# A mixture-of-experts kernel: moving one more store behind the last load, cutting the last weight load into whole rows, and storing the last result in one piece

## The chip, the cores and the metric

The kernel runs on one core of a Trainium2 chip. The time is the device time of one execution in microseconds (us); the figure before the change is the median of four runs. One further execution was profiled, and all durations below are from that one.

## The reference

Eight experts, each with its own tokens, weights and biases. Everything is float32.

```python
# x (8, 256, 512)  w1 (8, 512, 2048)  w2 (8, 2048, 512)  b1 (8, 2048)  b2 (8, 512)
def reference(x, w1, w2, b1, b2):
    h = np.matmul(x, w1) + b1[:, np.newaxis, :]
    h = np.maximum(h, 0)
    return (np.matmul(h, w2) + b2[:, np.newaxis, :]).astype(np.float32)
```

## The kernel before

For each expert e the kernel forms a hidden layer and then an output. `first_product(e)` (L108) multiplies `w1` with the transposed tokens in 16 blocks of 128 hidden rows, four matmuls each, and ScalarE applies bias and ReLU into `hT[e]` in fp16. `second_product(e)` (L151) starts two accumulators of 128 tokens x 512 columns with the bias `b2` and adds 16 hidden blocks (j = 0 to 15) to each. `store` (L134) copies the first accumulator to SBUF on VectorE and the second on ScalarE.

The main loop (L243) runs stages s = 0 to 10: stage s computes the first product of expert s and the second product of expert s - 3 (`LAG`). So stage 8 has the second product of expert 5, stage 9 that of expert 6 and stage 10 that of expert 7; these three stages have no first product.

**The ring.** All weight loads, the later token loads and seven of the eight stores are issued by GpSimd (POOL) into one DMA queue, q0, in the order of the list `ring` (L221 to L241). The loads change float32 into fp16 on the way. `flush(e)` (L130) issues the store of a finished expert, 512 KB, from that same list. The issue instruction of a flush waits on POOL until both copies of that expert are done, and everything later in the list waits behind it. There are eight semaphores for these transfers in turn, so each issue also waits until the eighth transfer before it has landed.

The end of the list before the change is: the load of w2 of expert 6 in two halves of 1 MB, flush 3, then the w2 of expert 7 in eight pieces (L232 to L236), then flush 5 and flush 6. Flush 4 stands behind the first piece (L237, L238), because expert 4 is not in `LATE = (5, 6)`. The eight pieces cover these rows j and columns: 0-4, 4-7, 7-10 and 10-12 over all 512 columns, then 12-14 and 14-16 over columns 0 to 320, then 12-14 and 14-16 over columns 320 to 512. A row is 512 float32 numbers in memory and 512 fp16 numbers (1 KB) in SBUF per partition, so a whole-row piece has one contiguous stretch per partition, and a column piece has one stretch per row and partition.

Expert 7 has four accumulators instead of two: columns 0 to 320 in two of them, columns 320 to 512 in two others. When rows 14-16 of the first 320 columns have been added, `store` copies these and SyncE (SP) issues a store of 320 KB (L149). The other 192 columns follow as two stores of 96 KB, one on SyncE (L142) and one on ScalarE's queue (L143). These three go through other DMA queues, q1 (SyncE) and q10 (ScalarE).

Output tiles of 512 columns rotate over three buffers (L48); those of the last expert have buffers of their own.

Of the kernel before, what the change touches and what calls it, by code (L numbers as in the profile page):

```python
# [11 lines left out]
def kernel(  # L12
# [9 lines left out]
    nc = tc.nc  # L22
    fp32 = mybir.dt.float32
    fp16 = mybir.dt.float16
    E, T, H = x.shape
    M = w1.shape[2]
    P = 128
    nTB = T // P
    nKC = H // P
    nJ = M // P  # L30
    HL = 320
    LAG = 3
    LATE = (5, 6)
    RING = (0, 1, 2, 3, 4) + LATE
    PARTS = {}
    nXF32 = 2

    def ordered(ins):
        return tc.keep_in_program_order(ins)

    singles = ctx.enter_context(tc.tile_pool(name="singles", bufs=1))
    w1_pool = ctx.enter_context(tc.tile_pool(name="w1", bufs=3))
    w2_pool = ctx.enter_context(tc.tile_pool(name="w2", bufs=3))
    w2t_pool = ctx.enter_context(tc.tile_pool(name="w2t", bufs=1))
    x_pool = ctx.enter_context(tc.tile_pool(name="xp", bufs=4))
    xT_pool = ctx.enter_context(tc.tile_pool(name="xTp", bufs=2))
    hT_pool = ctx.enter_context(tc.tile_pool(name="hT", bufs=LAG + 2))
    out_pool = ctx.enter_context(tc.tile_pool(name="outp", bufs=3))  # L48
    psum_x = ctx.enter_context(tc.tile_pool(name="psum_x", bufs=1, space=bass.MemoryType.PSUM))
    psum_h = ctx.enter_context(tc.tile_pool(name="psum_h", bufs=3, space=bass.MemoryType.PSUM))  # L50
    psum_o = ctx.enter_context(tc.tile_pool(name="psum_o", bufs=2, space=bass.MemoryType.PSUM))
# [3 lines left out]
    ones1 = singles.tile([1, P], fp16)  # L55
    b2_sb = singles.tile([1, E * H], fp16)
# [6 lines left out]
    w2_sb = [None] * E  # L63
    hT = [None] * E
# [14 lines left out]
    def load_w2(e):  # L79
        src = w2[e].rearrange("(p j) h -> p j h", j=nJ)  # L80
        w2_sb[e] = []
        t = w2_pool.tile([P, nJ, H], fp16, tag="w2", name="w2sb")
        step = nJ if e < E - 2 else nJ // 2
        for lo in range(0, nJ, step):
            ordered(nc.gpsimd.dma_start(out=t[:, lo : lo + step, :], in_=src[:, lo : lo + step, :]))  # L85
            w2_sb[e].append((lo, lo + step, 0, H, t[:, lo : lo + step, :]))

    def load_w2_piece(e, lo, hi, c0, c1):
        t = w2t_pool.tile([P, hi - lo, c1 - c0], fp16, tag=f"w2_{lo}_{c0}", name=f"w2_{lo}_{c0}")
        src = w2[e].rearrange("(p j) h -> p j h", j=nJ)  # L90
        ordered(nc.gpsimd.dma_start(out=t, in_=src[:, lo:hi, c0:c1]))  # L91
        if w2_sb[e] is None:
            w2_sb[e] = []
        w2_sb[e].append((lo, hi, c0, c1, t))

    def transposes(e):
        pt = psum_x.tile([P, nKC, T], fp16, tag="psx", name="psx")
# [33 lines left out]
        dst, src = pending.pop(e)  # L131
        ordered(nc.gpsimd.dma_start(out=dst, in_=src))  # L132

    def store(e, po, c0, c1, split):  # L134
        w = c1 - c0
        pool = out_pool if w == H else singles
        out_sb = pool.tile([P, nTB, w], fp32, tag=f"out{c0}_{w}", name=f"out{w}")
        nc.vector.tensor_copy(out=out_sb[:, 0, :], in_=po[0])  # L138
        nc.scalar.copy(out=out_sb[:, 1, :], in_=po[1])  # L139
        dst = out[e].rearrange("(p tb) h -> p tb h", tb=nTB)[:, :, c0:c1]  # L140
        if split and c1 == H:
            nc.sync.dma_start(out=dst[:, 0, :], in_=out_sb[:, 0, :])  # L142
            nc.scalar.dma_start(out=dst[:, 1, :], in_=out_sb[:, 1, :])  # L143
        elif e in RING:
            pending[e] = (dst, out_sb)
        else:
            step = P // PARTS.get(e, 1)
            for lo in range(0, P, step):
                nc.sync.dma_start(out=dst[lo : lo + step], in_=out_sb[lo : lo + step])  # L149

    def second_product(e):  # L151
        if e < E - 1:
            blocks = [(0, H, psum_o, "po")]
        else:
            blocks = [(0, HL, psum_o, "po"), (HL, H, psum_h, "ph")]
        acc = {}
        for c0, c1, pool, tag in blocks:
            for tb in range(nTB):
                t = pool.tile(
                    [P, c1 - c0], fp32, tag=tag if tag == "ph" else f"{tag}{tb}", name=f"acc{tb}"  # L160
                )
                acc[c0, tb] = t
                ordered(nc.tensor.matmul(  # L163
                    out=t,
                    lhsT=ones1,
                    rhs=b2_sb[0:1, e * H + c0 : e * H + c1],
                    start=True,
                    stop=False,
                ))
        for lo, hi, p0, p1, t in w2_sb[e]:  # L170
            mine = [b for b in blocks if p0 <= b[0] and b[1] <= p1]
            for tb in range(nTB):
                for j in range(lo, hi):
                    for c0, c1, _, _ in mine:
                        ordered(nc.tensor.matmul(  # L175
                            out=acc[c0, tb],
                            lhsT=hT[e][:, j, tb * P : (tb + 1) * P],
                            rhs=t[:, j - lo, c0 - p0 : c1 - p0],
                            start=False,
                            stop=(j == nJ - 1),  # L180
                        ))
            if hi == nJ:
                for c0, c1, _, _ in mine:
                    store(e, [acc[c0, tb] for tb in range(nTB)], c0, c1, e == E - 1)

    x32 = singles.tile([P, nXF32, nTB, H], fp32)
    for e in range(nXF32):
# [4 lines left out]
        out=b2_sb,  # L192
        in_=b2.rearrange("e h -> (e h)").rearrange("(o f) -> o f", o=1),
# [10 lines left out]
    for j in range(nJ):  # L204
        for s in range(2):
            ordered(nc.tensor.matmul(  # L206
                out=pb[s * 64 : (s + 1) * 64, j, :, :],
                lhsT=b1_rows.rearrange("r (q j) -> r q j", j=nJ)[:, :, j],
                rhs=ident[0 : 2 * E, 0 : 2 * E],
                start=True,  # L210
                stop=True,
            ))
    for s in range(2):
        nc.vector.tensor_copy(  # L214
            out=b1T[s * 64 : (s + 1) * 64, :, :], in_=pb[s * 64 : (s + 1) * 64, :, :, s]
# [5 lines left out]
    ring = []  # L221
    for s in range(1, E + LAG - 1):
        if s < E:
            if s >= nXF32:
                ring.append((s - 2, load_x, (s,)))
            ring.append((s - 2, load_w1, (s,)))
        if s >= LAG:
            ring.append((s - 2, load_w2, (s - LAG,)))
        if s >= 2 * LAG:
            ring.append((s - 2, flush, (s - 2 * LAG,)))  # L230
    e = E - LAG - 1
    for piece in (  # L232
        (0, 4, 0, H), (4, 7, 0, H), (7, 10, 0, H), (10, 12, 0, H),
        (12, 14, 0, HL), (14, 16, 0, HL), (12, 14, HL, H), (14, 16, HL, H),
    ):
        ring.append((0, load_w2_piece, (E - 1,) + piece))  # L236
        if e in RING and e not in LATE:  # L237
            ring.append((e + LAG + 1, flush, (e,)))  # L238
            e += 1
    for e in LATE:  # L240
        ring.append((e + LAG + 1, flush, (e,)))  # L241

    for s in range(E + LAG):  # L243
        while ring and ring[0][0] <= s:
            _, put, args = ring.pop(0)
            put(*args)
        if s < E:
            first_product(s)
        if s >= LAG:
            second_product(s - LAG)  # L250
# [31 lines left out]
```

## Time and profile before

| what | value |
|---|---|
| median of 4 runs | 183.58 us (183.32 to 183.65) |
| the profiled execution, its own time | 183.52 us |
| its span, first to last instruction | 181.7 us |
| TensorE matmul busy | 137.5 us (76% of the span) |
| ScalarE busy | 62.8 us (35%) |
| VectorE busy | 13.3 us (7%) |
| packets of DMA queue q0 | 97.8% of 16 engines' span |
| mean TensorE clock granted | 0.927 |

The span is the time from the first to the last instruction on the core; the execution's own time is 1.8 us longer. A core has 16 DMA engines that work for all queues; the share of a queue says how much of their time its packets took. The rate in GB/s counts the bytes of a transfer at its SBUF (or output) side, so a load that halves float32 into fp16 reads twice that from memory. "us to landing" of a DMA is the time from the start of its issue instruction to its last completion count.

### The profile page before, as it was taken

Reading aid. Unit: us, or ns where it says so; the run is one execution under the profiler, and the core shown is the slowest. Engines: PE = TensorE matmul, PEld = TensorE weight load, DVE = VectorE, ACT = ScalarE, POOL = GpSimd, SP = SyncE. Lnnn points to the kernel's source line nnn. Section 1 sums busy time; section 2 is a strip of 40 time slices with the busy share of each in tenths; the row PEclk is TensorE's granted clock in tenths of the full one; section 3 lists DMA queues with packets and bytes.
Section 4 is the critical chain, followed back from the end, with each engine's and each line's share of the span. In section 5 each row is a group of like instructions: output and inputs, shape, how many; then the busy total and the mean of one; then the engine's idle time right before and its main releaser. Section 6 shows DMA issues by size and latency. Waiting matters only on the chain.

```text
span 181.7 us, 2204 instructions
## 1 busy us (share of the span) xinstructions
PE 137.5 (76%) x946; PEld 98.2 (54%) x946; DVE 13.3 (7%) x22; ACT 62.8 (35%) x138; POOL 22.1 (12%) x46
## 2 busy tenths in 40 slices
PE   0545969488380999749992999709999996999790
PEld 0534959488360855737482755708549642434570
DVE  0320101001000101010100101001010010101010
ACT  0022869568270330806063330903309601010000
POOL 7100030300200010111010000200004003113300
PEclk9999999999966599988999699985999999999997
DMA  5989998999899999999999999999899989999995
GB/s 178 294 177 233 231 224 180 209 252 215 191 231 227 213 195 231 197 225 213 231 227 184 224 231 227 177 285 216 191 231 218 283 191 278 211 243 284 216 281 188
DMA packets 7017, 40.58 MB, mean 223 GB/s; under 512 B 1216, under 2 KB 2256, under 8 KB 4960
## 3 DMA queue, kind: packets, MB, share of 16 engines
q0 software_dynamic: 5872, 38.81, 97.8%
q1 hardware_dynamic: 688, 0.95, 1.6%
q10 hardware_dynamic: 448, 0.69, 1.0%
q8 instruction: 7, 0.11, 0.2%
q14 instruction: 2, 0.02, 0.0%
HBM read 71.39 MB, written 4.19 MB: 416 GB/s over the span
## 4 chain that ended last, share of the span: by engine, by line
DMA 82%; PE 13%; POOL 2%; issue 1%; ACT 0%; POOLq 0%
DMA w2sb<-in_w_dram 39%; DMA x<-in_x_dram 24%; DMA w1sb<-in_w_dram 13%; PE ph L113 7%; DMA w<-in_w_dram 6%; PE acc L175 5%; PE psx L100 1%; POOL w1sb L75 1%; PE acc L163 0%; POOL b_sb L191 0%; POOL ident masks.py:199 0%; POOL w2sb L85 0%; POOL ident masks.py:197 0%; ACT out L139 0%; POOLq L266 0%
## 5 line engine op out<-in xcount | busy, mean ns | idle before, releaser
L113 PE MATMUL ph<-xT,w1sb 128*128 128x256 f16 x512 | 68.5, 300 | 11.8 <-DMA w1sb<-in_w_dram 11.8
L120 ACT ACTIVATE hT<-ph,b1T 128x256 f16<-128x256 f32 x128 | 57.0, 474 | 44.4 <-PE ph L113 44.1
L113 PEld LDWEIGHTS <-w1sb 128*128 128x128 f16 x512 | 61.7, 149 | 17.9 <-DMA w1sb<-in_w_dram 12.8
L175 PE MATMUL acc<-w2sb,hT 128*128 128x512 f16 x224 | 49.6, 379 | 1.6 <-DMA w2sb<-in_w_dram 1.6
L175 PEld LDWEIGHTS <-hT 128*128 128x128 f16 x288 | 27.1, 98 | 32.7 <-issue 6.6
L139 ACT COPY out<-acc 128x512 f32<-128x512 f32 (+2 forms) x9 | 4.9, 542 | 59.6 <-PE acc L175 59.6
L100 PE MATMUL psx<-ident,x 128*128 128x128 f16 x64 | 6.6, 264 | 18.6 <-DMA x<-in_x_dram 17.9
L100 PEld LDWEIGHTS <-x 128*128 128x128 f16 x64 | 5.1, 127 | 19.6 <-DMA x<-in_x_dram 18.8
L75 POOL DMA_DIRECT2D w1sb<-in_w_dram x8 | 4.4, 553 | 59.5 <-PE ph L113 58.7
L106 DVE COPY xT<-psx 128x1024 f16<-128x1024 f16 x8 | 5.5, 691 | 82.2 <-PE psx L100 82.2
L138 DVE COPY out<-acc 128x512 f32<-128x512 f32 (+2 forms) x9 | 5.7, 632 | 73.3 <-PE acc L175 73.3
L85 POOL DMA_DIRECT2D w2sb<-in_w_dram x8 | 4.3, 536 | 49.4 <-PE acc L175 49.4
L175 PE MATMUL acc<-w,hT 128*128 128x320 f16 (+1 forms) x64 | 7.8, 272 | 1.4 <-DMA w<-in_w_dram 1.3
L206 PE MATMUL pb<-ident,b_rows 16*64 16x16 f32 x64 | 3.7, 265 | 6.5 <-DMA b_rows<-in_b_dram 6.5
L206 PEld LDWEIGHTS pb<-ident,b_rows 16*64 16x64 f32 x64 | 3.6, 198 | 6.4 <-issue 6.4
L91 POOL DMA_DIRECT2D w<-in_w_dram x8 | 5.0, 622 | 12.0 <-DMA w2sb<-in_w_dram 8.9
L132 POOL DMA_DIRECT2D out_dram<-out x7 | 3.8, 542 | 21.7 <-ACT out L139 13.1
L120 ACT ACT_TABLE_LOAD x1 | 1.3, 1283 | 10.9 <-DVE b1T L214 10.9
L163 PE MATMUL acc<-b_sb,ones 1*128 1x512 f16 (+2 forms) x18 | 4.8, 355 | 0.0
L69 POOL DMA_DIRECT2D x<-in_x_dram x6 | 3.3, 545 | 7.2 <-DMA w2sb<-in_w_dram 5.0
L163 PEld LDWEIGHTS <-ones 1*128 1x128 f16 x18 | 1.1, 92 | 2.2 <-issue 2.1
L201 DVE CAST x<-x 128x1024 f16<-128x1024 f32 x2 | 1.4, 694 | 4.3 <-DMA x<-in_x_dram 4.3
(9 smaller groups left out, 2.6 us busy)
## 6 DMA issues: line engine op xcount, KB each, us to landing
w1sb<-in_w_dram POOLq DMA_DIRECT2D x8, 2048.0 KB, 33.6
w2sb<-in_w_dram POOLq DMA_DIRECT2D x6, 2048.0 KB, 45.6
out_dram<-out POOLq DMA_DIRECT2D x7, 512.0 KB, 27.9
w2sb<-in_w_dram POOLq DMA_DIRECT2D x2, 1024.0 KB, 24.6
x<-in_x_dram POOLq DMA_DIRECT2D x6, 256.0 KB, 38.9
w<-in_w_dram POOLq DMA_DIRECT2D x2, 384.0 KB, 19.1
x<-in_x_dram SPq DMA_DIRECT2D x1, 512.0 KB, 4.5
x<-in_x_dram ACTq DMA_DIRECT2D x1, 512.0 KB, 5.2
```

The lines of the kernel that those rows point to most:

```text
L75: ordered(nc.gpsimd.dma_start(out=w1_sb[e], in_=w1[e].rearrange("(p kc) m -> p kc m", kc=nKC)))
L85: ordered(nc.gpsimd.dma_start(out=t[:, lo : lo + step, :], in_=src[:, lo : lo + step, :]))
L91: ordered(nc.gpsimd.dma_start(out=t, in_=src[:, lo:hi, c0:c1]))
L100: ordered(nc.tensor.transpose(out=pt[:, kc, tb * P : (tb + 1) * P], in_=x16[e][:, tb, :].rearrange("p (q kc) -> p q kc", kc=nKC)[:, :, kc] ...
L106: nc.vector.tensor_copy(out=xT[e], in_=pt)
L113: ordered(nc.tensor.matmul(out=ph, lhsT=w1_sb[e][:, kc, :].rearrange("p (q j) -> p q j", j=nJ)[:, :, j], rhs=xT[e][:, kc, :], start=(kc == 0),
L120: nc.scalar.activation(out=hT[e][:, j, :], in_=ph, func=mybir.ActivationFunctionType.Relu, bias=b1T[:, j, e : e + 1], scale=1.0,)
L138: nc.vector.tensor_copy(out=out_sb[:, 0, :], in_=po[0])
L139: nc.scalar.copy(out=out_sb[:, 1, :], in_=po[1])
L163: ordered(nc.tensor.matmul(out=t, lhsT=ones1, rhs=b2_sb[0:1, e * H + c0 : e * H + c1], start=True, stop=False,))
L175: ordered(nc.tensor.matmul(out=acc[c0, tb], lhsT=hT[e][:, j, tb * P : (tb + 1) * P], rhs=t[:, j - lo, c0 - p0 : c1 - p0], start=False, sto ...
L206: ordered(nc.tensor.matmul(out=pb[s * 64 : (s + 1) * 64, j, :, :], lhsT=b1_rows.rearrange("r (q j) -> r q j", j=nJ)[:, :, j], rhs=ident[0 ...
```

## The change

Three edits, all at the end of the program.

1. `LATE` is (4, 5, 6) instead of (5, 6): flush 4 is issued behind the last piece of w2 of expert 7, ahead of flush 5 and flush 6.
2. The w2 of expert 7 comes in five pieces of whole rows (0-4, 4-8, 8-12, 12-14, 14-16) instead of eight, four of which were column pieces.
3. Expert 7 has two accumulators of 512 columns, as the other experts have, and its result is copied once and issued as one store of 512 KB by SyncE. Its output tile comes from the common pool, which has four buffers instead of three; the separate tiles of 320 and 192 columns go.

```diff
-    HL = 320
     LAG = 3
-    LATE = (5, 6)
-    RING = (0, 1, 2, 3, 4) + LATE
-    PARTS = {}
+    LATE = (4, 5, 6)
...
-    out_pool = ctx.enter_context(tc.tile_pool(name="outp", bufs=3))
+    out_pool = ctx.enter_context(tc.tile_pool(name="outp", bufs=4))
...
-    def load_w2_piece(e, lo, hi, c0, c1):
-        t = w2t_pool.tile([P, hi - lo, c1 - c0], fp16, tag=f"w2_{lo}_{c0}", name=f"w2_{lo}_{c0}")
+    def load_w2_piece(e, lo, hi):
+        t = w2t_pool.tile([P, hi - lo, H], fp16, tag=f"w2_{lo}", name=f"w2_{lo}")
...
-    def store(e, po, c0, c1, split):
...
+    def store(e, po):
+        out_sb = out_pool.tile([P, nTB, H], fp32, tag="out", name="out")
         nc.vector.tensor_copy(out=out_sb[:, 0, :], in_=po[0])
         nc.scalar.copy(out=out_sb[:, 1, :], in_=po[1])
-        dst = out[e].rearrange("(p tb) h -> p tb h", tb=nTB)[:, :, c0:c1]
-        if split and c1 == H:
-            nc.sync.dma_start(out=dst[:, 0, :], in_=out_sb[:, 0, :])
-            nc.scalar.dma_start(out=dst[:, 1, :], in_=out_sb[:, 1, :])
-        elif e in RING:
+        dst = out[e].rearrange("(p tb) h -> p tb h", tb=nTB)
+        if e < E - 1:
             pending[e] = (dst, out_sb)
         else:
-            step = P // PARTS.get(e, 1)
-            for lo in range(0, P, step):
-                nc.sync.dma_start(out=dst[lo : lo + step], in_=out_sb[lo : lo + step])
+            nc.sync.dma_start(out=dst, in_=out_sb)
...
-    e = E - LAG - 1
-    for piece in (
-        (0, 4, 0, H), (4, 7, 0, H), (7, 10, 0, H), (10, 12, 0, H),
-        (12, 14, 0, HL), (14, 16, 0, HL), (12, 14, HL, H), (14, 16, HL, H),
-    ):
-        ring.append((0, load_w2_piece, (E - 1,) + piece))
-        if e in RING and e not in LATE:
-            ring.append((e + LAG + 1, flush, (e,)))
-            e += 1
+    for lo, hi in ((0, 4), (4, 8), (8, 12), (12, 14), (14, 16)):
+        ring.append((0, load_w2_piece, (E - 1, lo, hi)))
     for e in LATE:
         ring.append((e + LAG + 1, flush, (e,)))
```

In `second_product` the list of column blocks goes: one bias matmul and 16 matmuls of 512 columns per accumulator are left for every expert, and `store` is called once at its end.

More of the change, by code (lines that the diff above doesn't have):

```diff
@@ L85, in load_w2 @@
             ordered(nc.gpsimd.dma_start(out=t[:, lo : lo + step, :], in_=src[:, lo : lo + step, :]))
-            w2_sb[e].append((lo, lo + step, 0, H, t[:, lo : lo + step, :]))
-    def load_w2_piece(e, lo, hi, c0, c1):
-        t = w2t_pool.tile([P, hi - lo, c1 - c0], fp16, tag=f"w2_{lo}_{c0}", name=f"w2_{lo}_{c0}")
+            w2_sb[e].append((lo, lo + step, t[:, lo : lo + step, :]))
+    def load_w2_piece(e, lo, hi):
+        t = w2t_pool.tile([P, hi - lo, H], fp16, tag=f"w2_{lo}", name=f"w2_{lo}")
         src = w2[e].rearrange("(p j) h -> p j h", j=nJ)
-        ordered(nc.gpsimd.dma_start(out=t, in_=src[:, lo:hi, c0:c1]))
+        ordered(nc.gpsimd.dma_start(out=t, in_=src[:, lo:hi, :]))
         if w2_sb[e] is None:
             w2_sb[e] = []
-        w2_sb[e].append((lo, hi, c0, c1, t))
+        w2_sb[e].append((lo, hi, t))
     def transposes(e):
@@ L132, in flush @@
         ordered(nc.gpsimd.dma_start(out=dst, in_=src))
-    def store(e, po, c0, c1, split):
-        w = c1 - c0
-        pool = out_pool if w == H else singles
-        out_sb = pool.tile([P, nTB, w], fp32, tag=f"out{c0}_{w}", name=f"out{w}")
+    def store(e, po):
+        out_sb = out_pool.tile([P, nTB, H], fp32, tag="out", name="out")
         nc.vector.tensor_copy(out=out_sb[:, 0, :], in_=po[0])
         nc.scalar.copy(out=out_sb[:, 1, :], in_=po[1])
-        dst = out[e].rearrange("(p tb) h -> p tb h", tb=nTB)[:, :, c0:c1]
-        if split and c1 == H:
-            nc.sync.dma_start(out=dst[:, 0, :], in_=out_sb[:, 0, :])
-            nc.scalar.dma_start(out=dst[:, 1, :], in_=out_sb[:, 1, :])
-        elif e in RING:
+        dst = out[e].rearrange("(p tb) h -> p tb h", tb=nTB)
+        if e < E - 1:
@@ L145, in store @@
             pending[e] = (dst, out_sb)
         else:
-            step = P // PARTS.get(e, 1)
-            for lo in range(0, P, step):
-                nc.sync.dma_start(out=dst[lo : lo + step], in_=out_sb[lo : lo + step])
+            nc.sync.dma_start(out=dst, in_=out_sb)
     def second_product(e):
[L152 to L169, printed above, removed]
@@ L170, in second_product @@
-        for lo, hi, p0, p1, t in w2_sb[e]:
-            mine = [b for b in blocks if p0 <= b[0] and b[1] <= p1]
+        po = []
+        for tb in range(nTB):
+            t = psum_o.tile([P, H], fp32, tag=f"po{tb}", name=f"po{tb}")
+            po.append(t)
+            ordered(nc.tensor.matmul(
+                out=t, lhsT=ones1, rhs=b2_sb[0:1, e * H : (e + 1) * H], start=True, stop=False,
+            ))
+        for lo, hi, t in w2_sb[e]:
             for tb in range(nTB):
                 for j in range(lo, hi):
[L174 to L184, printed above, removed]
+                    ordered(nc.tensor.matmul(
+                        out=po[tb],
+                        lhsT=hT[e][:, j, tb * P : (tb + 1) * P],
+                        rhs=t[:, j - lo, :],
+                        start=False,
+                        stop=(j == nJ - 1),
+                    ))
@@ L186 @@
+        store(e, po)
     x32 = singles.tile([P, nXF32, nTB, H], fp32)
```

## The prediction

> **What bounds the kernel now.** I read the queue table first, then the chain of waits, then the tail from 150 us on: TensorE's timeline, the landing of each transfer, and the stretches at the end.
>
> ```profile
> q0 software_dynamic: 5872, 38.81, 97.8%
> ...
> DMA 82%; PE 13%; POOL 2%; issue 1%; ACT 0%; POOLq 0%
> ...
> 164.28 11.49 DMA w<-in_w_dram
> 175.77 0.04 issue
> 175.81 1.51 PE acc L175 x12
> 177.32 0.02 issue
> 177.34 0.32 ACT out L139
> ```
>
> Queue q0 keeps the DMA engines busy for 97.8% of the span, and the chain is 82% DMA. The last link names a piece of w2, then twelve matmuls, then a copy. That link alone suggests a compute tail, so TensorE's own rows at the end come next (start, us busy, in brackets the idle time before):
>
> ```profile
> 160.59 7.08 PE L175 MATMUL acc<-w2sb,hT 128*128 128x512 f16 x32
> 167.60 0.61 PE L163 MATMUL acc<-b_sb,ones 1*128 1x320 f16 x4
> 168.14 1.92 PE L175 MATMUL acc<-w,hT 128*128 128x320 f16 x16
> 171.04 1.47 PE L175 MATMUL acc<-w,hT 128*128 128x320 f16 x12 [0.98 <-DMA w<-in_w_dram]
> 172.85 4.46 PE L175 MATMUL acc<-w,hT 128*128 128x320 f16 x36 [0.34 <-DMA w<-in_w_dram]
> ```
>
> TensorE waits only 1.3 us for the last pieces and ends at 177.3. It is close behind the loads, but there are stores still to come. DMA in stretches there (the last two figures are the DMA share and GB/s):
>
> ```profile
> 169.20:172.80 3.60, 2.33 (x20) 1.69 (x19) 0.00 (x0) 0.00 (x0) 1.10 (x2) 1.00 1.10 207
> 176.80:177.40 0.60, 0.51 (x5) 0.26 (x3) 0.22 (x1) 0.23 (x2) 0.00 (x0) 1.00 1.03 423
> 177.40:178.20 0.80, 0.00 (x0) 0.00 (x0) 0.14 (x1) 0.26 (x1) 0.00 (x0) 1.00 0.53 215
> 178.30:179.40 1.10, 0.00 (x0) 0.00 (x0) 0.00 (x0) 0.00 (x0) 0.00 (x0) 0.86 0.99 364
> ```
>
> Loads run at 207 GB/s, q0's stores at 423, the small stores of the end at 364. From 177.4 to 178.2 the engines are half idle. The trace's sixteen completion counts of a transfer explain this: those of flush 6 come in two groups, eight at 177.69 to 178.05 and eight at 178.29 to 179.35. Half of the engines are about 1.1 us ahead, and one is the last every time. Each landing below is that last engine's. Adding the time to landing to the issue start (six such rows; a piece of w2 is "w"):
>
> ```profile
> out_dram<-out POOLq DMA_DIRECT2D x1, 512.0 KB, 17.3
> ...
> w<-in_w_dram POOLq DMA_DIRECT2D x1, 96.0 KB, 8.6
> ...
> out_dram<-out POOLq DMA_DIRECT2D x1, 512.0 KB, 7.7
> ...
> out_dram<-out SPq DMA_DIRECT2D x1, 320.0 KB, 3.2
> out_dram<-out SPq DMA_DIRECT2D x1, 96.0 KB, 3.0
> out_dram<-out ACTq DMA_DIRECT2D x1, 96.0 KB, 2.7
> ```
>
> Flush 4 issued at 151.87 lands at 169.16, the piece of rows 4-7 issued at 152.39 at 171.00, the last piece issued at 168.13 at 176.77, flush 6 issued at 171.61 at 179.35. The stores of the last result, issued at 177.00, 177.67 and 177.69, land at 180.23, 180.70 and 180.43; the span ends at 181.74. The other landings, to two decimals: flush 3 165.57, rows 0-4 167.85, rows 7-10 172.81, rows 10-12 174.06, the 320-column pieces 174.88 and 175.77, the first 192-column piece 176.25, flush 5 178.08. On that last engine the intervals follow without a hole, so the sum of transfers sets the end. TensorE sets it only if the last store arrives late.
>
> **The change, part by part.** I start both sums at 167.85, where rows 0-4 land: nothing that q0 carries before differs.
>
> Before, from 167.85: flush 4 1.31; rows 4-10 (768 KB) 3.65; rows 10-12 (256 KB) 1.25; the 320-column pieces 1.71; the 192-column pieces 1.00; flush 5 1.31; flush 6 1.27; what is left of the last 512 KB 1.35. Together 12.85, which gives 180.70.
>
> After, *loads*: rows 4-8 and 8-12 are 1024 KB, at the rate of rows 4-10 that is 3.65 x 1024/768 = 4.87. Rows 12-14 and 14-16 are two pieces exactly like rows 10-12: 2.50. Together 7.37 against 7.61 before. The 0.24 saved is the price of the column pieces: 512 KB took 2.71 in them, against 2.50 in whole rows (the other 0.03 is a slightly slower row for the same rows). From below: the interval of rows 0-4, 2.28 for 512 KB, would give 3 x 2.28 = 6.84, another 0.53 less. I take 7.37, because 2.28 follows a long flush 3 (1.57), and the two together equal 2.5 + 1.3. From above: no gain, 7.61.
>
> *Stores*: flush 4 moves, and costs its 1.31 at the new place as at the old; flushes 5 and 6 stay at 1.31 and 1.27. Moving by itself is worth nothing in this sum. It makes the loads land 1.31 earlier.
>
> *The last store*: 512 KB in stretches of 4 KB instead of 1280 and 768 bytes. The nearest row is flush 6, 1.27; the other end is the 1.35 of before. I take 1.30. In the sum: 7.37 + 3.89 + 1.30 = 12.56, landing at 180.41, 0.29 earlier.
>
> *Does the last store come in time?* The pieces land at 170.29, 172.72, 173.97 and 175.22. TensorE starts expert 7 at 167.60: two bias matmuls of 512 columns, 0.60 (the same row of expert 6); then 32 matmuls at 7.08/32 = 0.221. Rows 0-4: 168.20 to 169.97; rows 4-8: 170.3 to 172.1; rows 8-12: 172.75 to 174.5; rows 12-16, already landed by then or on the way: to 176.3. Before, it ended at 177.32. ScalarE's copy of 512 columns takes 0.59 and starts 0.06 later, VectorE's of 0.69 starts two matmuls earlier; so SyncE issues at 177.0, as it did before. That time its first packets started 1.26 later, at 178.26, which on the fast engines leaves the same hole as now. The last engine is at work on flush 6 until its landing at 167.85 + 7.37 + 3.89 = 179.1. So the store is queued about half a microsecond before that engine needs it (its packets end some 0.35 ahead of the landing). Without any queue before it the store would take 1.26 + 1.3 + 0.35 and land near 179.9, below the 180.4 of the sum.
>
> *What waits for what on POOL.* Before, the pieces of rows 4-7 and later stood behind flush 4, which waited 13.1 us for ScalarE's copy until 151.87; now they wait only for the transfer eight before (landings at 142.0, 143.3, 153.0, 154.3). That is worth nothing: q0 held transfers until 167.85 in either order. Flushes 4, 5 and 6 are now issued near 159.3, 164.3 and 168.4 (the first two behind landings at 159.06 and 164.00, the third behind ScalarE's copy ending at 168.34), 8 us and more ahead of the 175.2 at which the loads land. If that cover were gone, a flush would cost its delay directly.
>
> *Rest*: 68 rows fewer on TensorE and two copies of 512 columns for four smaller ones are inside the path above. Four output buffers for all eight experts: the copies of expert 7 wait for flush 3, landed at 165.57, ten microseconds earlier. Nothing.
>
> The profiled execution then goes from 183.52 to 183.23. Its time lies 0.06 under the median of the runs, so the forecast for a median is 183.3.
>
> **Two rules against the trace.** The 192-column pieces write 384 bytes at a time, and 192 KB took 1.00 us, 5.2 us per MB; the 640-byte pieces took 5.3. The Trainium skill ("DMA: Bandwidth & Descriptors", Specifications) says that transfers under 512 bytes fall below line rate through a read-modify-write; by that the pieces dropped here would have stood out, and dropping them would save far more than 0.24. The trace shows no step there. The same page (Anatomy of one DMA) fits a transfer as 2.0 us plus bytes at 436 GB/s. That speaks against one big store at the end: 177.0 + 3.2 = 180.2, against 177.7 + 2.2 = 179.9 for the small ones before, so 0.3 later and 183.9 in all. The rows of before (2.7 to 3.2 us, behind other stores) show the queue, not the fixed part, deciding.
>
> **The rivals.**
> 1. *The last store is exposed* (slower). One store of 512 KB needs all copies; before, 320 KB set out 0.67 ahead of the rest. The row for 512 KB issued by SyncE is the load of x at the start, 4.5 us: 177.0 + 4.5 = 181.5, 0.8 later than 180.70, or 184.4. It decides when SyncE issues later than about 177.5; from there each tenth costs a tenth. For it: TensorE ends only half a microsecond ahead. Against: that row shared the engines with another x load and w1.
> 2. *The order and the shape of pieces make nothing* (same). If the column pieces cost only what their bytes cost and the last store stays at 1.35, the sum is 12.85 again: 183.5 to 183.65. For it: 0.24 is a difference of intervals each read from one execution.
> 3. *Whole rows run at the best interval* (faster). With 6.84 for the loads the sum is 12.03 and the end 179.88; TensorE would end near 175.8 and its store near 179.4, still hidden. 182.7 to 182.8.
>
> **How the numbers follow.** The forecast case has 0.52, rival 1 0.22, rival 2 0.14, rival 3 0.12. A measurement can tell about 0.2%, 0.37 us here, from no change: faster is below 183.21, slower above 183.95. The forecast, 183.3 with its own range 183.0 to 183.6, lies near the lower edge: of its 0.52, 0.22 below, 0.28 within, 0.02 above. Rival 1: 0.17 slower, 0.05 within. Rival 2: 0.11 within, 0.03 slower. Rival 3: all faster. Faster 0.34, same 0.44, slower 0.22. The range goes from 182.8 (rival 3) to 184.2, inside rival 1 whose far end is 184.4.
>
> **What would show it.** Last piece landing near 175.2; matmuls ending near 176.3; SyncE's issue near 177.0; flush 6 landing near 179.1; the last store near 180.4; the rate of q0's stores at 420 GB/s over 3.9 us. It is wrong if TensorE ends after 176.8, if a flush is issued after the loads have landed, if whole-row pieces of 256 KB take other than 1.25, or if the last store lands over 0.4 after the last engine is done with flush 6 plus 1.3.

## The result and the profile after

The changed kernel takes 183.08 us (median of 44 runs, 182.71 to 183.77) against 183.53 us before (median of 65 runs). The ratio is 0.9974, with a 95% interval of 0.9969 to 0.9978: 0.26% faster, or 0.45 us by the medians (0.4 to 0.6). The forecast was 183.3.

The profiled execution of the changed kernel took 182.71 us, the lowest of its 44 runs; its span is 180.9 us. So the 0.8 us between the two profiles is more than the change brings as a rule, and the first thing to do is to see where that surplus sits.

The queue table and the chain of the changed kernel (the chain's columns are start, us, what):

```profile
q0 software_dynamic: 4928, 38.81, 97.4%
...
114.45 38.34 DMA w2sb<-in_w_dram
152.80 0.04 issue
152.84 8.75 PE po L152 x32
161.59 0.53 PE po L146 x2
162.13 7.01 PE po L152 x32
169.14 0.53 PE po L146 x2
169.67 7.03 PE po L152 x32
176.70 0.03 ACTq L134
176.73 0.04 issue
176.77 0.59 ACT out L134
```

The DMA queue is as full as before, but from 152.8 us on the chain is now matmuls up to the last copy, and no piece of w2 of expert 7 appears in it. TensorE's timeline and SyncE's issue say the same from the other side: expert 7's 32 matmuls run without a wait.

```profile
152.84 8.75 PE L152 MATMUL po<-w2sb,hT 128*128 128x512 f16 x32 [2.35 <-DMA w2sb<-in_w_dram]
161.53 0.60 PE L146 MATMUL po<-b_sb,ones 1*128 1x512 f16 x2
162.06 7.08 PE L152 MATMUL po<-w2sb,hT 128*128 128x512 f16 x32
169.07 0.60 PE L146 MATMUL po<-b_sb,ones 1*128 1x512 f16 x2
169.60 7.08 PE L152 MATMUL po<-w,hT 128*128 128x512 f16 x32
...
177.38 0.35 SPq L139 DMA_DIRECT2D out_dram<-out  x1
```

Expert 5's 32 matmuls took 8.75 us where they took 7.07 before. That is the granted clock, 0.59 in the first stretch of the next view (the third figure from the right), and it pushes the last store's issue to 177.38. No run ties it to the change. Of the 14 kernels profiled here, five have it at this place, and in these TensorE had stood still for 2.05 to 2.58 us just before; the other nine had waited 1.77 us or less there and took 7.07 or 7.08. (Elsewhere longer waits can go without it: 3.25 us ahead of 37.2 in the profile of before.) The changed kernel with flush 3 late as well, below, waited 1.12 us and issued its last store at 176.17.

```profile
152.80:156.20 3.40, 3.36 (x10) 1.30 (x10) 0.00 (x0) 0.00 (x0) 1.05 (x2) 0.59 1.09 246
...
177.40:178.20 0.80, 0.00 (x0) 0.00 (x0) 0.00 (x0) 0.00 (x0) 0.00 (x0) 1.00 0.40 164
178.30:179.40 1.10, 0.00 (x0) 0.00 (x0) 0.00 (x0) 0.00 (x0) 0.00 (x0) 1.00 0.99 406
```

From 178.3 to 179.4 the engines move 406 GB/s, where it was 364. Their busy share is 0.99 instead of 0.86, so they stand idle less and are not faster while busy; both stretches still hold the end of flush 6. The hole from 177.4 to 178.2 is still there. Issues to landing, in order: rows 8-12 (issued 143.41), rows 14-16 (154.35), flush 4 (159.46), flush 5 (164.42), flush 6 (170.10), the last store (177.38).

```profile
w<-in_w_dram POOLq DMA_DIRECT2D x1, 512.0 KB, 28.9
...
w<-in_w_dram POOLq DMA_DIRECT2D x1, 256.0 KB, 20.5
...
out_dram<-out POOLq DMA_DIRECT2D x1, 512.0 KB, 16.7
...
out_dram<-out POOLq DMA_DIRECT2D x1, 512.0 KB, 13.0
...
out_dram<-out POOLq DMA_DIRECT2D x1, 512.0 KB, 8.6
out_dram<-out SPq DMA_DIRECT2D x1, 512.0 KB, 2.6
```

To two decimals: rows 0-4 land at 167.43, rows 14-16 at 174.86, flush 4 at 176.18, flush 5 at 177.42, flush 6 at 178.66, the last store at 180.02. The last store before landed at 180.70. Of these 0.68 us, 0.42 are already there when rows 0-4 land, ahead of anything the change touches. Before, one engine was late by itself: flush 3's completion counts there end 165.06, 165.11, 165.24, 165.57; in the changed kernel they end 165.02, 165.02, 165.03, 165.04. From rows 0-4 to the end it is 12.85 before and 12.59 after, 0.26 less.

### The profile page after: what moved, and what is told of

Its sections match the earlier page's. It is cut to its first block, busy times and chain, and to the rows that moved or that the text cites. A ratio compares the mean times of both kernels' runs of the same rounds, so it can differ in the third digit from the quotient of the medians.

```text
span 180.9 us, 2129 instructions
## 1 busy us (share of the span) xinstructions
PE 138.4 (76%) x912; PEld 95.6 (53%) x912; DVE 13.2 (7%) x21; ACT 62.7 (35%) x137; POOL 19.7 (11%) x43
## 4 chain that ended last, share of the span: by engine, by line
DMA 58%; PE 24%; issue 9%; another core or an unknown queue 4%; POOL 2%; ACT 0%; POOLq 0%; ACTq 0%
DMA x<-in_x_dram 25%; DMA w2sb<-in_w_dram 21%; PE po L152 16%; DMA w1sb<-in_w_dram 13%; PE ph L110 6%; PE po L146 1%; PE psx L97 1%; POOL w2sb L82 1%; POOL w1sb L72 1%; ACT out L134 0%; POOL out_dram L129 0%; POOL b_sb L166 0%; POOL ident masks.py:199 0%; POOL ident masks.py:197 0%
## 5 line engine op out<-in xcount | busy, mean ns | idle before, releaser
L152 PE MATMUL po<-w2sb,hT 128*128 128x512 f16 x224 | 51.2, 388 | 2.3 <-DMA w2sb<-in_w_dram 2.3
L152 PEld LDWEIGHTS <-hT 128*128 128x128 f16 x256 | 24.9, 100 | 35.3 <-issue 8.0
L134 ACT COPY out<-po 128x512 f32<-128x512 f32 x8 | 4.7, 589 | 60.4 <-PE po L152 60.4
L133 DVE COPY out<-po 128x512 f32<-128x512 f32 x8 | 5.5, 691 | 73.2 <-PE po L152 73.2
L152 PE MATMUL po<-w,hT 128*128 128x512 f16 x32 | 7.1, 379 | 0.0
L146 PE MATMUL po<-b_sb,ones 1*128 1x512 f16 x16 | 4.8, 379 | 0.0
L88 POOL DMA_DIRECT2D w<-in_w_dram x5 | 2.7, 533 | 14.9 <-DMA w2sb<-in_w_dram 13.4
```

The source lines that it names most:

```text
L146: ordered(nc.tensor.matmul(out=t, lhsT=ones1, rhs=b2_sb[0:1, e * H : (e + 1) * H], start=True, stop=False,))
L152: ordered(nc.tensor.matmul(out=po[tb], lhsT=hT[e][:, j, tb * P : (tb + 1) * P], rhs=t[:, j - lo, :], start=False, stop=(j == nJ - 1),))
```

## The experiments

Two theories stood at the start. Theory 1 is the prediction's: the end is the sum of transfers on the last DMA engine, so only the shape of the pieces (and a little the shape of the last store) counts, and moving flush 4 is worth nothing. Theory 2: the issue of the last store sets the end, and flush 4 behind the last piece is what makes it early. Each kernel is compared with the kernel before, timed again beside it on the same chip (medians there: 183.48 to 183.51).

**Flush 4 moved, nothing else.**

```diff
-    LATE = (5, 6)
-    RING = (0, 1, 2, 3, 4) + LATE
+    LATE = (4, 5, 6)
+    RING = (0, 1, 2, 3) + LATE
```

> Only flush 4 goes behind the last piece; column pieces and three small stores as before. Theory 1 (the end is the sum of transfers on the last DMA engine, as in the prediction): the sum is unchanged, so no change, 183.5 us, within 0.1 of before. Theory 2 (the issue of the last store sets the end, and moving flush 4 makes it earlier): last store issued about 1 us earlier, 0.3 us or more faster, 183.2.

Measured: 183.54 us, ratio 1.0001 (0.9992 to 1.0009). The last stores were issued at 175.76 to 176.53, over 1 us earlier than before, and it bought nothing. SyncE's issues, and the landings of the three stores:

```profile
175.76 0.61 SPq L149 DMA_DIRECT2D out_dram<-out  x1
176.42 0.59 SPq L142 DMA_DIRECT2D out_dram<-out  x1
...
out_dram<-out SPq DMA_DIRECT2D x1, 320.0 KB, 4.5
out_dram<-out SPq DMA_DIRECT2D x1, 96.0 KB, 4.3
out_dram<-out ACTq DMA_DIRECT2D x1, 96.0 KB, 4.0
```

What they gained at the issue they lost waiting: 4.0 to 4.5 us to landing where it was 2.7 to 3.2. The last landing is at 180.75, against 180.70. Theory 1 holds here and theory 2 falls.

**Whole-row pieces, nothing else.**

```diff
-        (0, 4, 0, H), (4, 7, 0, H), (7, 10, 0, H), (10, 12, 0, H),
-        (12, 14, 0, HL), (14, 16, 0, HL), (12, 14, HL, H), (14, 16, HL, H),
+        (0, 4, 0, H), (4, 8, 0, H), (8, 12, 0, H), (12, 14, 0, H), (14, 16, 0, H),
```

> Only the pieces of w2 of expert 7 change to whole rows 4, 4, 4, 2, 2; flush 4 stays behind the first piece, accumulators and stores stay split in 320 and 192 columns. Theory 1: the loads save 0.2 us, 183.3. Theory 2: the last piece lands near 176.5 and both column blocks end with it, so the 320-column store is issued near 178.0 instead of 177.0 and the last one near 178.3: 0.3 us slower, 183.8.

Measured: 183.81 us, ratio 1.0021 (1.0010 to 1.0032): slower, as theory 2 had it. Both column blocks now end with the last piece; the three stores were issued at 177.96, 178.29 and 178.36 (SyncE's 96 KB came ahead of its 320 KB), and the last of them landed 2.65 later, at 181.01, though flush 6 had landed at 179.03. This profile has the low clock in expert 5 too (8.73 us), but it is not what made the issue late: TensorE waits for rows 8-12, which land at 173.97, and half of expert 7's matmuls are left then.

**Whole rows and one store, flush 4 left in its old place.** Against the changed kernel this undoes the move alone.

```diff
-    LATE = (4, 5, 6)
+    LATE = (5, 6)
...
         ring.append((0, load_w2_piece, (E - 1, lo, hi)))
+        if lo == 0:
+            ring.append((8, flush, (4,)))
```

> Whole-row pieces and one store of 512 KB, but flush 4 stays behind the first piece. Theory 1: the full forecast gain of 0.29 us, 183.2, because moving flush 4 costs and saves nothing. Theory 2: last piece lands near 176.5, matmuls end near 177.45, SyncE issues near 178.1 and the store lands 2.65 later, near 180.75: no gain, 183.5 to 183.7.

Measured: 183.70 us, ratio 1.0011 (1.0003 to 1.0020), 0.62 above the changed kernel. TensorE's last rows, the issue, its landing and the DMA stretches around it:

```profile
170.21 3.63 PE L152 MATMUL po<-w,hT 128*128 128x512 f16 x16
174.29 3.61 PE L152 MATMUL po<-w,hT 128*128 128x512 f16 x16 [0.45 <-DMA w<-in_w_dram]
...
178.59 0.35 SPq L139 DMA_DIRECT2D out_dram<-out  x1
...
out_dram<-out SPq DMA_DIRECT2D x1, 512.0 KB, 2.6
...
178.00:179.00 1.00, 0.00 (x0) 0.00 (x0) 0.26 (x1) 0.57 (x1) 0.00 (x0) 1.00 0.31 127
179.00:180.00 1.00, 0.00 (x0) 0.00 (x0) 0.00 (x0) 0.00 (x0) 0.00 (x0) 1.00 0.58 238
```

TensorE waits for rows 8-12, and has 16 matmuls left when they land; the store goes out at 178.59, and the DMA engines run dry before its data reaches them (0.31 and 0.58 busy in two whole microseconds). Here too expert 5 ran at the low clock (8.75 us), as in the profile of the changed kernel, so these two are a fair pair: the wait for rows 8-12 is what differs, and the issue is 1.21 us later. All sixteen engines report the store between 181.06 and 181.23. So narrow a spread (0.17 to 0.18 us) is seen in the five profiles in which the issue decides, as the last table shows; in the others the counts spread over 0.33 to 1.77 us.

So both theories are right, each in its place. **Theory 3: the end is the later of two things, the last engine being through with its queue (flush 6 landed, plus 1.2 to 1.4 for the last 512 KB), and the issue of the last store plus 2.65.** The 2.65 is that of a store of 512 KB (or of the 320 KB above, behind the two of 96 KB); the two of 96 KB took 1.82 and 1.89.

**One store and flush 4 moved, column pieces kept.** The pieces are those of before, added into column ranges of the two full accumulators.

```diff
...
-    for lo, hi in ((0, 4), (4, 8), (8, 12), (12, 14), (14, 16)):
-        ring.append((0, load_w2_piece, (E - 1, lo, hi)))
+    for piece in (
+        (0, 4, 0, H), (4, 7, 0, H), (7, 10, 0, H), (10, 12, 0, H),
+        (12, 14, 0, 320), (14, 16, 0, 320), (12, 14, 320, H), (14, 16, 320, H),
+    ):
+        ring.append((0, load_w2_piece, (E - 1,) + piece))
```

> Flush 4 behind the last piece and one store of 512 KB, but the eight pieces of before, four of them column pieces (they add into column ranges of the two full accumulators). Theory 1: only the last store's 0.05 us is gained, 183.45. Theory 2: as for the whole change, since the store is issued near 177.0 either way, 183.1 to 183.2. The difference to the changed kernel is the price of column pieces: forecast 0.24 us.

Measured: 183.51 us, ratio 1.0002 (0.9991 to 1.0013). Whole rows in place of the column pieces are thus worth 0.43 us by the medians (183.51 to 183.08). By the traces, rows 0-4 to the last piece take 7.71 here, 7.70 with flush 4 moved alone, and 7.43 in the changed kernel: 0.27 to 0.28.

**Flush 4 moved and whole rows, three small stores kept** (the two diffs above, of the first and second run, together).

> Flush 4 behind the last piece and whole-row pieces; only the split into 320 and 192 columns with three small stores stays. Theory 3, from the first four runs: the end is the later of two things, the last DMA engine being through with its queue, and the issue of the last store plus 2.65 us. In the run with whole rows alone the third store was issued 0.70 after the last matmul; from matmuls ending near 176.7 that gives 180.05, no later than the engines' own end: nearly all of the gain, 183.1 to 183.2. Rival: the single store itself brings the gain, so this stays at 183.4 to 183.5.

Measured: 183.16 us, ratio 0.9982 (0.9973 to 0.9990). Rows 0-4 to the last piece: 7.43 again. The single store is not what brings the gain: by the medians it is worth 0.08 here, which is within the uncertainty.

**One store, nothing else** (the kernel of the column pieces above with flush 4 put back behind the first piece).

> The kernel before with one change alone: the last result in one store of 512 KB; column pieces stay, flush 4 stays behind the first piece. Matmuls end near 177.3, the store is issued near 178.0 and lands 2.65 later, 180.65, beside the 180.70 of before: no change, 183.5. Theory 1 of the first runs gives 183.45, so only a loss of 0.2 or more would speak against both.

Measured: 183.48 us, ratio 0.9998 (0.9989 to 1.0007). Issued at 178.06, landed at 180.69 on all engines within 0.17 us: the late store and the queues (flush 6 at 179.37) here end at the same time.

These six and the whole change make a small table (medians, us; flush 4's place in the columns). For whole rows it decides the sign; for column pieces it does nothing.

| pieces, stores | flush 4 early | flush 4 moved |
|---|---|---|
| column pieces, three stores | 183.5 (before) | 183.54 |
| column pieces, one store | 183.48 | 183.51 |
| whole rows, three stores | 183.81 | 183.16 |
| whole rows, one store | 183.70 | 183.08 (the change) |

**All of w2 of expert 7 in column pieces**, to enlarge the price four times.

```diff
-        (0, 4, 0, H), (4, 7, 0, H), (7, 10, 0, H), (10, 12, 0, H),
-        (12, 14, 0, 320), (14, 16, 0, 320), (12, 14, 320, H), (14, 16, 320, H),
+        (0, 4, 0, 320), (0, 4, 320, H), (4, 8, 0, 320), (4, 8, 320, H),
+        (8, 12, 0, 320), (8, 12, 320, H), (12, 14, 0, 320), (12, 14, 320, H),
+        (14, 16, 0, 320), (14, 16, 320, H),
```

> As the kernel with flush 4 moved and one store, but all of w2 of expert 7 comes in column pieces of 320 and 192 columns (ten pieces), not only its last four rows. If column pieces cost 0.27 us per 512 KB more than whole rows, 2 MB of them end 0.8 later than 512 KB of them: 184.3. If what separated the changed kernel from that one was not the shape of pieces but the engine that happened to be last, 183.5.

Measured: 184.06 us, ratio 1.0027 (1.0017 to 1.0038), 0.98 above the changed kernel for 2 MB, 0.245 per 512 KB; against the kernel with 512 KB of column pieces only 0.55 for the other 1.5 MB, 0.18 per 512 KB. That is below the 184.3 expected, so the price per 512 KB is 0.18 to 0.25 here and not 0.27, but it is far from the 183.5 of a chance engine: the price is that of the column pieces. Their number (ten instead of five) is not the likely reason, since in the changed kernel's profile two whole-row pieces of 256 KB take 2.51 us where one of 512 KB takes 2.46.

**Flush 3 behind the last piece as well.**

```diff
-    LATE = (4, 5, 6)
+    LATE = (3, 4, 5, 6)
...
-    out_pool = ctx.enter_context(tc.tile_pool(name="outp", bufs=4))
+    out_pool = ctx.enter_context(tc.tile_pool(name="outp", bufs=5))
...
-        if s >= 2 * LAG:
+        if s >= 2 * LAG and s - 2 * LAG not in LATE:
```

> The changed kernel with flush 3 behind the last piece too (five output buffers). The loads land 1.3 us earlier again. If the last engine's queue sets the end, no change against the changed kernel, 183.1; if the issue of the last store still sets it in most executions, up to 0.3 faster, 182.8.

Measured: 183.01 us, ratio 0.9972 (0.9962 to 0.9983); not to be told from the changed kernel. The last store was issued at 176.17 and landed 4.2 us later: it waited in the queues. With three stores of cover the cover is enough.

**More instruction fetches.** In the trace, besides the kernel's own queues, q8 carries packets of 16 KB, seven in either profile, each 0.88 to 0.98 us long.

```diff
+    pd = psum_x.tile([P, nJ, E, 2], fp32, tag="psx", name="pd")
+    for _ in range(256):
+        ordered(nc.tensor.matmul(
+            out=pd[0:16, 0, :, :], lhsT=ident[0:16, 0:16], rhs=ident[0:16, 0:16], start=True, stop=True,
+        ))
     pb = psum_x.tile([P, nJ, E, 2], fp32, tag="psx", name="pb")
```

> The changed kernel with 256 idle matmuls of 16 columns at the start of TensorE's program, where TensorE waits for the first weights (their result is not used). The trace shows 16 KB instruction fetches of 0.95 us, each on one DMA engine; these matmuls should add about two to the seven. If the end is that of the last engine, and a fetch lands on an engine that is already behind, 183.4 to 184.0 and one engine's landings late by a further microsecond; if spread evenly, 0.1 us (183.2). If the fetches have nothing to do with the engines' lag, 183.1.

Measured: 190.22 us, ratio 1.0347 (1.0329 to 1.0366). As a price of fetches it fails: the idle matmuls were double what was counted on (512 matmuls, four more packets on q8), and TensorE had to stop for them.

```profile
q8 instruction: 11, 0.18, 0.3%
...
3.17 6.13 PE L180 MATMUL pd<-ident 16*16 16x16 f32 x223 [3.17 <-POOL ident masks.py:199]
11.58 3.57 PE L180 MATMUL pd<-ident 16*16 16x16 f32 x128 [2.28 <-issue]
17.50 3.57 PE L180 MATMUL pd<-ident 16*16 16x16 f32 x128 [2.35 <-issue]
23.70 1.04 PE L180 MATMUL pd<-ident 16*16 16x16 f32 x33 [2.63 <-issue]
```

Three times it stood still for 2.3 to 2.6 us; a q8 packet starts within 0.3 us of each stop (9.25, 15.21 and 21.28), so TensorE seems to have run through its instructions faster than they came. The first product began at 31.1, and the weight buffers came free so late that the DMA engines had a hole (5 GB/s in one of the 40 slices; nothing at all from 39 to 42 us). That start is the likely bulk of the 7 us.

The run does show something of the lag. Five packets came ahead of the hole, and in the last load there five completion counts are about 1 us late (eleven at 37.05 to 37.46, five at 38.29 to 38.66). The first weight load behind it, after the packet at 51.83, has fifteen counts at 53.16 to 53.56 and one at 54.49: the lag was gone. Only six of the eleven packets come after the hole, and six engines are behind at the end, flush 6's counts going from 184.04 to 184.50 for ten engines and from 185.46 to 186.18 for six.

**Work shifted between the engines.** On the kernel with flush 3 late too, 32 partitions of expert 5's result go out as four stores of 8 partitions.

```diff
+            hi = P
+            if e == 5:
+                hi = 96
+                for lo in range(hi, P, 8):
+                    nc.sync.dma_start(out=dst[lo : lo + 8], in_=out_sb[lo : lo + 8])
-            pending[e] = (dst, out_sb)
+            pending[e] = (dst[0:hi], out_sb[0:hi])
```

> The kernel with flushes 3 to 6 behind the last piece, but 32 of the 128 partitions of expert 5's result go out as four stores of 8 partitions issued by SyncE as soon as they are copied; flush 5 stores the other 96. In every profile so far eight engines end about 1 us behind the other eight. A store of 8 partitions has eight rows to give out, so it can reach at most eight engines. If those are the eight that are ahead, the others have two rows of 4 KB less each, 0.33 us, and the end comes 0.3 earlier than without: 182.7. If they are the eight that are behind, 0.3 later: 183.3 to 183.4. If the lag does not set the end, no change: 183.0.

Measured: 183.10 us, ratio 0.9977 (0.9967 to 0.9986): nothing gained on 183.01. In its profile the two groups of eight did run together (flush 6's counts go evenly from 177.26 to 178.98, with one at 179.27), but its last store was issued at 178.31, after matmuls of expert 5 at a reduced clock again (8.75 us). So a kernel was tried in which TensorE starts earlier, without and with that shift:

```diff
-        step = nJ if e < E - 2 else nJ // 2
+        step = nJ if e < E - 3 else nJ // 2
```

> The kernel with flushes 3 to 6 late, and w2 of expert 5 in two loads of 1 MB like expert 6's, so that TensorE can start its second product about 4.8 us earlier and the last three experts' matmuls have slack even where the clock is granted at half. If the last store's issue still limits some executions: up to 0.2 faster than without, 182.8. If the last engine's queue is all that counts: no change, 183.0.

> The same with 32 partitions of expert 5's result stored by SyncE in four stores of 8 partitions, as tried before. That kernel's profile had the eight engines evened out but its last store issued late, at 178.31, and landing 2.6 later on all engines. If that late issue is what kept it at 183.1, an early issue now lets the evened queues end earlier: 182.6 to 182.8. If not, 183.0 to 183.1 again.

Measured: 183.14 us, ratio 0.9979 (0.9965 to 0.9992), and 183.00 us, ratio 0.9974 (0.9965 to 0.9983). With stores issued at 176.27 and 176.18 neither is faster than the changed kernel. Evening out the groups left one engine last: flush 6's counts in the second end 178.53, 178.55, 178.82, 179.07. No version tried beats the changed kernel by more than the uncertainty.

Theory 3 against the profiles, us from the start of the span (one execution each):

| kernel | flush 6 landed | last store issued | issue + 2.65 | last landing |
|---|---|---|---|---|
| before | 179.35 | 177.69 | 180.34 | 180.70 |
| flush 4 moved | 179.38 | 176.53 | 179.18 | 180.75 |
| flushes 3 to 6 late | 179.16 | 176.17 | 178.82 | 180.40 |
| all column pieces | 179.81 | 177.23 | 179.88 | 181.00 |
| the change | 178.66 | 177.38 | 180.03 | 180.02 |
| one store only | 179.37 | 178.06 | 180.71 | 180.69 |
| whole rows only | 179.03 | 178.36 | 181.01 | 181.01 |
| whole rows, one store | 179.27 | 178.59 | 181.24 | 181.23 |
| flushes 3 to 6 late, work shifted | 179.27 | 178.31 | 180.96 | 180.93 |
| flush 4 moved, one store | 179.29 | 177.73 | 180.38 | 180.52 |
| flush 4 moved, whole rows | 178.84 | 176.95 | 179.60 | 180.19 |
| w2 of expert 5 in halves | 179.27 | 176.27 | 178.92 | 180.50 |
| the same, work shifted | 179.07 | 176.18 | 178.83 | 180.28 |
| more instruction fetches | 186.18 | 184.28 | 186.93 | 187.42 |

In the first four and the last five the landing is flush 6 plus 1.19 to 1.37; in the five between, the change itself among them, it is the issue plus 2.62 to 2.65. Before, and with flush 4 moved alone, the last store is one of 96 KB, so 2.65 is too much for it; the queues are the later of the two all the same. In the profile of the change the low clock had made the issue late, so an execution without it would be expected to end with the queues.

## Why the prediction was right, and by how much it was not

- **What bounds the kernel.** Right: the sum of transfers on the last engine. Moving flush 4 alone and leaving the rest changed the issue by over 1 us and the time by nothing.
- **The loads.** Forecast 7.37 from rows 0-4 to the last piece, measured 7.43; pieces of 256 KB forecast 1.25, measured 1.30 and 1.22. The column pieces' price was forecast 0.24 and is 0.27 by the traces, 0.18 to 0.245 per 512 KB by the enlarged run. Over all profiles the loads take 7.61 to 7.71 with the column pieces of before and 7.22 to 7.44 with whole rows, so the sign is not that of one execution.
- **The flushes.** Forecast 3.89 for three, measured 3.80. POOL issued them at 159.46, 164.42 and 170.10, all ahead of the loads' landing. The third came 1.7 late, behind the low clock. The text's "8 us and more ahead" did not fit its own numbers (175.2 less 168.4 is 6.8); 4.8 was measured, and was enough.
- **The last store.** Forecast 1.30 behind flush 6. Measured 1.24, 1.23 and 1.19 where one store waited in the queues, 1.35 to 1.37 with three small ones. The saving is 0.1 to 0.2 by the traces, not 0.05; by the medians it is 0.02 to 0.11, which can hardly be told from nothing. In the changed kernel's profile it is 1.36, because there the issue decides. (The 364 GB/s that the text read as the rate of the small stores is an average over a busy share of 0.86; the sum did not use it.)
- **The sum.** Forecast 12.56, measured 12.59. That these agree to 0.03 is partly luck: the loads came 0.06 over, the flushes 0.09 under, and the last store 0.06 over for a reason outside the sum. The forecast gain of 0.29 is nonetheless too small: 0.45 by the medians. The text gave no change that can be told the largest chance, 0.44, and "faster", below 183.21, 0.34; 183.08 lies there, and inside the forecast's own 183.0 to 183.6. The mis-sized terms are the loads' 0.24 and the last store's 0.05: 0.27 and 0.1 to 0.2 by the traces, and 0.38 to 0.43 for whole rows alone by the medians (183.54 to 183.16, and 183.51 to 183.08). What makes the medians' figure larger than the traces' by about 0.1 stays open; each trace is one execution, and the changed kernel's runs alone spread over 1 us.
- **"Moving by itself is worth nothing".** Right as a term of the sum, and shown. But the text gave it no part in the gain, and it has one: it is the cover without which whole rows lose 0.2 to 0.3 us. The condition stood there as the question whether the last store comes in time; the half microsecond of slack in the answer was not asked for with flush 4 in its old place.
- **TensorE's end and the issue.** Forecast 176.3 and 177.0, in the profile 176.7 and 177.38, because of the granted clock (0.59 for 3.4 us), not because of a wait. The slack of half a microsecond was used up: the store and the queues ended together.
- **Rival 1, the exposed store.** It did not happen with the change as a whole, but whole rows without the move are just this. Its price was too high: 4.5 us came from a load that shared the engines; a store of 512 KB alone takes 2.64 from issue to landing. The forecast's own figure for that, 2.9 (1.26 + 1.3 + 0.35), was too high as well: its first packets start 0.85 after the issue in the changed kernel's profile (178.23), not 1.26.
- **Rival 2** falls with the runs on column pieces, **rival 3** with the whole-row loads: 7.36 to 7.44 from rows 0-4 to the last piece (flush 4 left out where it lies between) in all profiles with whole rows but one (7.22, where work was shifted), never 6.84. The pieces of rows 4-8 and 8-12 took 2.40 to 2.53 in these, and 2.46 in the change.
- **The two rules.** The Trainium skill, "DMA: Bandwidth & Descriptors", Specifications, puts transfers under 512 bytes below line rate. In the run with all column pieces, 192 KB in 384-byte writes took 1.03 to 1.08 us (5.5 to 5.8 us per MB), 320 KB in 640-byte writes behind them 1.60 to 1.65 (5.1 to 5.3), and whole rows 4.9 per MB: smaller writes cost more, with no jump at 512. Its fit for one DMA (Anatomy of one DMA, measured there for transfers issued by GpSimd) would give 3.2 us for the last store, an estimate. SyncE issued this one, and 2.64 was measured, so the late store costs less than that; and in no row of the table of medians is one store slower than three.

## What to carry to other kernels

At the end of a kernel bound by DMA there are two clocks, the queues' end and the last store's issue plus its own latency; an edit to one is worth nothing while the other is later, so write both down before costing an edit. Stores kept behind the last load buy no DMA time, but they cover the compute after that load, and make it possible to choose the load's pieces for the DMA's sake (whole rows) and not for an early start of the last store. Look at the spread of the sixteen completion counts of the last store: in these runs 0.2 us meant a late issue, and over 1 us meant queues; in between it told neither.

## What the hardware showed unasked

The sixteen DMA engines do not run abreast, and instruction fetches coincide with it. In the profile of before, the first q8 packet of 16 KB starts at 21.17 and takes 0.89 us; the next weight load's counts are fifteen at 25.00 to 25.21 and one at 26.24. After the second packet (36.76) two engines are late, after the third (63.59) three, after the fourth (87.94) four, and by the end, after seven, seven or eight are, by 0.9 to 1.4 us in the profiles. The run with more fetches fits: behind its hole the engines were abreast again, and the six packets that came then left six engines late. That each packet holds up the engine that carries it is argued from these times, not isolated by a run. As long as the queues are never empty a late engine stays late, since in these profiles every transfer of the ring has a count from each of the sixteen, so the end of a DMA-bound kernel depends on which engines were hit.

TensorE can, it seems, run through its instructions faster than they are fetched: 256 short matmuls in the source stopped it three times for 2.3 to 2.6 us, each time beside a q8 packet. The profile itself names no cause for these stops.
